# Last FFN by seven block products for gate and up, convolution sums in PSUM, weight lo parts on GpSimd

## The chip, the cores and the metric

The kernel runs on one core of a Trainium2 chip. The metric is the device time of one execution in microseconds. Three executions of the kernel before took 2322.36, 2325.06 and 2325.65 us; their median is 2325.06 us. The engines are called PE (TensorE), DVE (VectorE), ACT (ScalarE), POOL (GpSimd) and SP (SyncE, which issues all DMAs here).

## The reference

A trunk of two layers over 1024 tokens of 1024 channels, all in float32. Layer 0 has a hybrid mixer (gated linear attention beside stick-breaking attention), layer 1 a conformer convolution module; behind each stands a gated FFN of width 2816. Cut to what the change touches:

```python
def conformer_conv(h, w_pw1, b_pw1, w_dw, b_dw, ln_g, ln_b, w_pw2, b_pw2):
    a = h @ w_pw1 + b_pw1
    u = a[..., :D_MODEL] * jax.nn.sigmoid(a[..., D_MODEL:])
    u = depthwise_causal_conv(u, w_dw, width=31) + b_dw
    u = layer_norm(u, ln_g, ln_b)
    return jax.nn.silu(u) @ w_pw2 + b_pw2

def swiglu(h, wg, wu, wd):
    return (jax.nn.silu(h @ wg) * (h @ wu)) @ wd

for layer in range(2):
    h = h + mixer(rms_norm(h, mix_norm[layer]))
    h = h + swiglu(rms_norm(h, ffn_norm[layer]), ffn_w_gate[layer], ffn_w_up[layer], ffn_w_down[layer])
```

(`depthwise_causal_conv`, `layer_norm` and `mixer` stand for several lines of the reference.)

## The kernel before, in words

Every large product is made of three matmuls. A float32 operand is split into a high part, rounded to the format fp32r (a copy on ACT), and a low part, the remainder (a subtraction on DVE); `split` (line 95) does both, `parts` (line 167) does it for a piece of weights, and `mm3` (line 205) adds hi x hi, hi x lo and lo x hi into one PSUM tile. A matmul has 128 rows of the contraction, 128 stationary columns and 512 moving ones.

The tokens are worked in two halves of 512. The residual lies in SBUF as eight token tiles `xres` of 128 x 1024. A norm (`norm_half`, line 142) scales the tokens, transposes them on PE and leaves hi and lo parts with the channels on the partitions, eight blocks of 128 channels ("k").

An FFN of one half of the tokens is a list of steps (`ffn_steps`, line 238). A chunk step takes 128 of the 2816 hidden columns: 24 matmuls for gate (`pg`) and 24 for up (`pu`), then Silu on ACT, the product `s` on DVE (line 261), and its split into `a`. After each group of four chunks two `down` steps (line 211), one for each half of the output columns, multiply the group's activations by `ffn_w_down` and add the PSUM tile `po` to `xres` on DVE (line 230). In the first layer's FFN of the first half the groups have two chunks.

A step is a pair (weights, body). `run` (line 186) traces the weights of a step, that is their DMA, the hi copies and the lo subtractions, one such step ahead of its body. The tile framework then orders the instructions of each engine at build time by a simulated timeline: what is ready and stands earliest in the program goes first, so the matmuls of neighbouring steps can mix. On the chip each engine runs its list in that order.

Layer 1 and the FFNs that surround it are one list of steps, which the last `run` of the kernel gets. For the second half of the tokens the order is: the first pointwise step `p1[0]`, the norm for `f10` (the last FFN's first half), then the other seven pointwise steps and 21 steps of `f10`, between which 32 pieces of the depthwise convolution are spread (`conv_steps`, line 897: eight channel blocks, four pieces each, a piece being up to eight taps, each tap one DVE instruction of line 908 on 128 x 512, accumulating in an SBUF tile `cv`); then six steps of `f10` with the twelve steps of the LayerNorm between them (`layer_norm`, line 915: four for the statistics of the token tiles, eight for transposing back, swish and split), the rest of `f10` but four steps, the four steps of the second pointwise product (`pw2`), the norm for `f11` (the last FFN's second half), the last four steps of `f10`, and `f11`. The stores of the output follow the steps that finish each half.

PSUM has eight buffers of 128 x 512. In layer 1 they are shared out as three of tag "a" (gate, up, pointwise), three of "b" (down) and two of "n" (norms and transposes). Raw weights have two buffers of 128 x 2048, split weights eight of 128 x 1024, for the whole kernel. The bias of the second pointwise product is added to `xres` on POOL (line 963), the only large work POOL has.

The lines that the rows name: L97 hi copies (ACT), L98 lo subtractions (DVE), L146 the norm's scaling, L207 to L209 the three matmuls of `mm3`, L230 the add of `po` to `xres`, L887 the gated pointwise output `u`, L908 a tap, L930 to L936 the LayerNorm's statistics.

Of the kernel before, what the change touches and what calls it, by code (L numbers as in the profile page):

```python
# [25 lines left out]
NF = DFF // P  # L26
EPS = 1e-6
# [12 lines left out]
def trunk(ctx, tc, x, mix_norm, ffn_norm, hy_w_in, hy_w_gate2, hy_b_gate, hy_gla_norm,  # L40
# [8 lines left out]
    raw_p = ctx.enter_context(tc.tile_pool(name="raw", bufs=2))  # L49
    ws_p = ctx.enter_context(tc.tile_pool(name="ws", bufs=8))  # L50
    dram = ctx.enter_context(tc.tile_pool(name="dram", bufs=1, space=DRAM))

# [7 lines left out]
    identr = const.tile([P, P], F32R, name="identr")  # L60
    nc.scalar.copy(identr, ident)
    maskr = const.tile([P, P], F32R, name="maskr")
    hones = const.tile([P, P], F32, name="hones")
    nc.vector.memset(hones, 0.0)
    nc.vector.memset(hones[0:64, 0:64], 1.0 / 64.0)
    nc.vector.memset(hones[64:128, 64:128], 1.0 / 64.0)

    # vectors, 128 channels to a row, transposed on chip into columns
# [34 lines left out]
    small = ctx.enter_context(tc.tile_pool(name="small", bufs=2))  # L103

    def inv_sqrt(y, ss, scale, name):
        """y = 1 / sqrt(ss * scale + eps), by Newton's iteration."""
# [12 lines left out]
    def x_tile(name, dt=F32):  # L119
        return hold.tile([P, 1056], dt, name=name, tag="x", bufs=8)  # L120
# [6 lines left out]
    def norm_stats(xt, junk, name):  # L127
        """1 / RMS of four token tiles."""
# [13 lines left out]
    def norm_half(xt, xn, rs, gcol, ps, pstag, name, muls):  # L142
        """Four token tiles scaled (into xn); returns the transposed hi and lo parts [D chunk, 8, 512]."""
# [11 lines left out]
    def load_cols(w, c0, name, n=256):  # L155
        """n columns of a weight with 1024 rows."""
# [4 lines left out]
    def load_rows(w, r0, n, j, name):  # L161
        """n chunks of 128 rows of a weight with 1024 columns, half j of the columns."""
# [4 lines left out]
    def parts(raw_ap, name, shape=(P, NK, P)):  # L167
        hi = ws_p.tile(list(shape), F32R, name=f"wh_{name}", tag="ws")
        lo = ws_p.tile(list(shape), F32R, name=f"wl_{name}", tag="ws")
        split(hi, lo, raw_ap)  # L170
        return hi, lo

    # A step is a function, or a pair (weights, body) whose weights are traced one such step ahead.
    def interleave(main, filler):
        """The main steps in order, with the filler steps spread evenly behind them."""
# [29 lines left out]
    def mm3(ps, sh, sl, mh, ml, first, last):  # L205
        """ps += s^T m by the three leading products of the hi and lo parts."""
        nc.tensor.matmul(ps, sh, mh, start=first, stop=False)  # L207
        nc.tensor.matmul(ps, sh, ml, start=False, stop=False)  # L208
        nc.tensor.matmul(ps, sl, mh, start=False, stop=last)  # L209
# [803 lines left out]
```

## Time and profile before

| | us |
|---|---|
| median of three executions | 2325.06 |
| lowest and highest | 2322.36, 2325.65 |
| profiled execution, span from the first to the last instruction | 2319.9 |
| PE busy | 2290.3 |
| DVE busy | 1591.3 |
| ACT busy | 922.4 |
| POOL busy | 32.9 |

Of the profiled execution only the span is given, and no time of its own beside it; the span is 5.2 us shorter than the median of the three. "Busy" is time in which an instruction's record is open on the engine. Matmul records overlap, so the spacing of their starts tells more than their length. "Idle before" in a row is the time its engine stood still just before, and the arrow names what ended it.

### The profile page before, as it was taken

How to read it: one execution, taken by the hardware profiler on the slowest of the kernel's cores; microseconds unless marked ns; L12 is line 12 of the kernel's file. 1: busy time of each engine (PE TensorE's matmuls, PEld its weight loads, DVE VectorE, ACT ScalarE, POOL GpSimd, SP SyncE). 2: the span in 40 equal slices, each digit the busy share in tenths (PEclk: the TensorE clock that was granted, in tenths of full speed). 3: DMA queues.
4: the chain of work that ended last, by engine and by line, in shares of the span. 5: the costliest groups of instructions: out<-in, count | busy, mean ns of one | idle time of the engine just before them, and what ended most of it. 6: DMA issues, size and time to landing. Idle time of an engine off the chain costs nothing.

```text
span 2319.9 us, 27940 instructions
## 1 busy us (share of the span) xinstructions
PE 2290.3 (99%) x10866; PEld 1899.1 (82%) x10866; DVE 1591.3 (69%) x2486; ACT 922.4 (40%) x1506; POOL 32.9 (1%) x39
## 2 busy tenths in 40 slices
PE   7999999999999999999999999999999999999999
PEld 6788888788888887788888888888888888888887
DVE  6687764877788656588888856789998545334334
ACT  6465545655565324523222245422222424222221
POOL 0000000000000001000000002000000000000000
PEclk9999999999999999999999999999999999999999
DMA  6254454233343235233222322322322223322322
GB/s 207 97 163 141 167 188 141 76 98 118 100 131 111 68 103 181 73 97 103 91 93 89 109 91 82 109 86 96 109 91 91 91 92 127 109 91 92 108 84 80
DMA packets 206387, 253.74 MB, mean 109 GB/s; under 512 B 8709, under 2 KB 156272, under 8 KB 206254
## 3 DMA queue, kind: packets, MB, share of 16 engines
q1 hardware_dynamic: 206254, 251.95, 33.5%
q8 instruction: 85, 1.39, 0.2%
q14 instruction: 48, 0.39, 0.1%
HBM read 230.95 MB, written 20.97 MB: 109 GB/s over the span
## 4 chain that ended last, share of the span: by engine, by line
PE 95%; DMA 2%; DVE 2%; ACT 1%; issue 0%; SPq 0%; ACTq 0%; DVEq 0%
PE po L207 9%; PE po L209 9%; PE po L208 9%; PE pu L207 7%; PE pu L209 7%; PE pu L208 7%; PE pg L207 7%; PE pg L209 7%; PE pg L208 7%; PE pp L208 2%; PE pp L207 2%; PE pp L209 2%; PE po L652 2%; PE wt L634 1%; PE z L617 1%; PE z L613 1%
## 5 line engine op out<-in xcount | busy, mean ns | idle before, releaser
L908 DVE SCALAR_TENSOR_TENSOR cv<-u,wd,cv 128x512 f32<-128x512 f32 x480 | 358.1, 749 | 9.9
L230 DVE TENSOR_TENSOR xr<-xr,po 128x512 f32<-128x512 f32 x296 | 202.1, 684 | 168.8 <-PE po L209 168.0
L207 PE MATMUL po<-wh_d,a 128*128 128x512 f32 x704 | 277.8, 395 | 1.7 <-DVE xr L230 1.6
L207 PE MATMUL pg<-hh_f,wh_g 128*128 128x512 f32 x704 | 275.8, 392 | 3.6 <-DVE s L260 3.6
L208 PE MATMUL pg<-hl_f,wh_g 128*128 128x512 f32 x704 | 276.6, 393 | 0.0
L209 PE MATMUL pg<-hh_f,wl_g 128*128 128x512 f32 x704 | 275.8, 392 | 0.0
L209 PE MATMUL po<-wh_d,a 128*128 128x512 f32 x704 | 275.5, 391 | 0.0
L208 PE MATMUL pu<-hl_f,wh_u 128*128 128x512 f32 x704 | 275.4, 391 | 0.0
L208 PE MATMUL po<-wl_d,a 128*128 128x512 f32 x704 | 275.2, 391 | 0.0
L209 PE MATMUL pu<-hh_f,wl_u 128*128 128x512 f32 x704 | 275.2, 391 | 0.0
L207 PE MATMUL pu<-hh_f,wh_u 128*128 128x512 f32 x704 | 275.0, 391 | 0.0
L97 ACT CAST wh_g<-raw_g 128x1024 fp32r<-128x1024 f32 x88 | 92.8, 1054 | 348.4 <-PE po L208 226.2
L97 ACT CAST wh_d<-raw_d 128x1024 fp32r<-128x1024 f32 x88 | 92.5, 1053 | 252.0 <-PE pu L208 116.7
L98 DVE TENSOR_TENSOR wl_g<-raw_g,wh_g 128x1024 fp32r<-128x1024 f32 x88 | 107.6, 1223 | 88.0 <-ACT wh_g L97 83.8
L207 PEld LDWEIGHTS po<-wh_d,a 128*128 128x128 f32 x704 | 132.3, 188 | 31.4 <-DVE xr L230 4.0
L207 PEld LDWEIGHTS pg<-hh_f,wh_g 128*128 128x128 f32 x704 | 132.6, 188 | 30.8 <-DVE s L260 3.8
L209 PEld LDWEIGHTS po<-wh_d,a 128*128 128x128 f32 x704 | 132.2, 188 | 27.8
L209 PEld LDWEIGHTS pg<-hh_f,wl_g 128*128 128x128 f32 x704 | 132.7, 189 | 27.0
L208 PEld LDWEIGHTS pu<-hl_f,wh_u 128*128 128x128 f32 x704 | 132.3, 188 | 27.3
L261 DVE TENSOR_TENSOR s<-s,pu 128x512 f32<-128x512 f32 x88 | 60.5, 687 | 137.1 <-PE pu L209 134.5
L208 PEld LDWEIGHTS pg<-hl_f,wh_g 128*128 128x128 f32 x704 | 132.6, 188 | 26.7
L209 PEld LDWEIGHTS pu<-hh_f,wl_u 128*128 128x128 f32 x704 | 132.2, 188 | 27.0
(318 smaller groups left out, 4300.3 us busy)
## 6 DMA issues: line engine op xcount, KB each, us to landing
raw_g<-in_ffn_w_gate_dram SPq DMA_DIRECT2D x44, 1024.0 KB
raw_u<-in_ffn_w_up_dram SPq DMA_DIRECT2D x44, 1024.0 KB
raw_d<-in_ffn_w_down_dram SPq DMA_DIRECT2D x30, 1024.0 KB
raw_p<-in_cv_w_pw_dram SPq DMA_DIRECT2D x16, 1024.0 KB
raw_d<-in_ffn_w_down_dram SPq DMA_DIRECT2D x28, 512.0 KB
raw_wo<-in_hy_w_out_dram SPq DMA_DIRECT2D x8, 1024.0 KB
raw_q<-in_cv_w_pw_dram SPq DMA_DIRECT2D x8, 1024.0 KB
kr<-k_d SPq DMA_DIRECT2D x48, 128.0 KB
```

The lines of the kernel that those rows point to most:

```text
L97: nc.scalar.copy(hi, src)
L98: nc.vector.tensor_sub(lo, src, r32(hi))
L207: nc.tensor.matmul(ps, sh, mh, start=first, stop=False)
L208: nc.tensor.matmul(ps, sh, ml, start=False, stop=False)
L209: nc.tensor.matmul(ps, sl, mh, start=False, stop=last)
L230: nc.vector.tensor_add(xt[i][:, cs], xt[i][:, cs], po)
L261: nc.vector.tensor_mul(s, s, pr[1])
L613: nc.tensor.matmul(z, qs[:, sub(i)], kh[:, s0:s0 + w], start=True, stop=False)
L617: nc.tensor.matmul(z, qs[:, sub(i)], kl[:, s0:s0 + w], start=False, stop=True)
L634: nc.tensor.transpose(pt[:, col:col + P], wrow[bi][:, P * j:P * j + P], ident)
L652: nc.tensor.matmul(po[:, lo_c:256], st["v"][j // 4][:, j % 4, e, :], m[:, 256 * jj + lo_c:256 * jj + 256], start=(last and jj == 0 and m i ...
L908: i = nc.vector.scalar_tensor_tensor(acc, u[:, j:j + TH], wd[:, c, j:j + 1], acc, op0=ALU.mult, op1=ALU.add)
```

## The change

For gate and up of the last FFN the whole product is seen as a 2 x 2 by 2 x 2 block product: blocks of 512 channels, 512 tokens and 1408 hidden columns (11 chunks of 128). b11, b21, b12 and b22 are the normed tokens: the first index is the half of the channels, the second the half of the tokens. It is done with seven block products and additions (the Winograd form of Strassen's method) in place of eight. Two of the seven are on the first half of the tokens and the first half of the hidden columns; they are made in `f10`, which keeps 11 of its 22 chunks. The first of these two products is copied out of PSUM by ACT and stored to DRAM (`m1_d`) while the second is accumulated onto it. The other five come in a new last stage, for eleven pairs of chunks (f and 11 + f), gate and up: `pair_weights` forms four sums of weight blocks on DVE and splits them, `pair_products` makes the five products of 12 matmuls, `pair_down` the down product of the pair. For token tiles 0 to 3 the down product of chunk f was already made in `f10`, so only chunk 11 + f is left.

The new stage has pools of its own; raw and split weights' pools of the earlier stages are closed before it. The order of its steps is gate f, the two down steps of pair f - 1, up f, gate f + 1. At its start `token_sums` and `token_sum4` form the sums of the token blocks on DVE.

In the stage before, the sums of the convolution lie in PSUM (two buffers of tag "cv", and "a" and "b" have two each instead of three), with a copy to SBUF by ACT after the last tap; the lo parts of weights are subtracted on GpSimd; and `f10` being shorter, the convolution's pieces are spread over 16 steps (7 pointwise steps and 9 of `f10`) in place of 28, the LayerNorm's steps over 4 in place of 6. Small tables move into the first stage's pool, and `xres` tiles are 1024 instead of 1056 columns wide.

```diff
-    def split(hi, lo, src, scale=None):
+    def split(hi, lo, src, scale=None, eng=None):
         if scale is None:
             nc.scalar.copy(hi, src)
-            nc.vector.tensor_sub(lo, src, r32(hi))
+            (eng or nc.vector).tensor_sub(lo, src, r32(hi))
...
     def parts(raw_ap, name, shape=(P, NK, P)):
...
-        split(hi, lo, raw_ap)
+        split(hi, lo, raw_ap, eng=weight_engine[0])
...
-    def ffn_steps(l, h, hT, xt, ps, ft, act, use_silu, group):
+    def ffn_steps(l, h, hT, xt, ps, ft, act, use_silu, group, last=NF, early=None):
...
+            if early is not None:
+                for k0 in (0, 4):
+                    for t, (pm, w) in enumerate(zip(pr, ws)):
+                        for k in range(k0, k0 + 4):
+                            mm3(pm, w[0][:, k, :], w[1][:, k, :], hT()[0][:, k, :], hT()[1][:, k, :],
+                                k == 0, k == k0 + 3, skip_group_check=True)
+                        if k0 == 0:
+                            m1 = ft(f"m{t}{nm}")
+                            nc.scalar.copy(m1, pm)
+                            nc.sync.dma_start(early[t, f], m1)
...
+        weight_engine[0] = nc.gpsimd
-        ftp = es.enter_context(tc.tile_pool(name="ft2", bufs=3))
+        ftp = es.enter_context(tc.tile_pool(name="ft2", bufs=4))
...
-            BUFS = {"a": 3, "b": 3, "n": 2}
+            BUFS = {"a": 2, "b": 2, "n": 2, "cv": 2}
...
                 if j0 == 0:
-                    cT[h, c] = cvp.tile([P, TH], F32, name=f"cv{h}{c}", tag="cv")
-                acc = cT[h, c]
+                    sums[h, c] = ps.tile([P, TH], F32, name=f"cs{h}{c}", tag="cv")
+                acc = sums[h, c]
...
+                if j1 == TAPS:
+                    cT[h, c] = cvp.tile([P, TH], F32, name=f"cv{h}{c}", tag="cv")
+                    nc.scalar.copy(cT[h, c], acc)
...
-        f10 = ffn_steps(1, 0, lambda: hT["f10"], xres, ps, ft, act, True, 4)
-        f11 = ffn_steps(1, 1, lambda: hT["f11"], xres, ps, ft, act, True, 4)
+        f10 = ffn_steps(1, 0, lambda: hT["f10"], xres, ps, ft, act, True, 4, NP, m1_d)
...
-               norm_step(0, ffng[1], "f10")] + interleave(p1[1:] + f10[:21], conv_steps(1))
-            + interleave(f10[21:27], ln1) + f10[27:-4] + pw2(1, s1) + [norm_step(1, ffng[1], "f11")]
-            + f10[-4:] + [lambda: store(0, 0), lambda: store(0, 1)]
-            + f11[:-1] + [lambda: store(1, 0), f11[-1], lambda: store(1, 1)])
+               norm_step(0, ffng[1], "f10")] + interleave(p1[1:] + f10[:-8], conv_steps(1))
+            + interleave(f10[-8:-4], ln1) + pw2(1, s1) + [norm_step(1, ffng[1], "f11")] + f10[-4:])
+    weights_es.close()
+    with ExitStack() as es:
+        weight_engine[0] = nc.vector
+        raw_p = es.enter_context(tc.tile_pool(name="raw3", bufs=5))
+        ws_p = es.enter_context(tc.tile_pool(name="ws3", bufs=6))
...
+            BUFS = {"a": 6, "b": 2}
...
+        def token_sums(k):
+            r1, r3, r2 = [whole(b, k, nm) for b, nm in ((b11, "b11"), (b12, "b12"), (b22, "b22"))]
+            nc.vector.tensor_sub(r1, r3, r1)
+            nc.vector.tensor_sub(r3, r2, r3)
+            nc.vector.tensor_sub(r2, r2, r1)
+            for t, r in ((t2, r2), (t3, r3), (t1, r1)):
+                split(t[0][:, k, :], t[1][:, k, :], r)
...
+        def pair_weights(w, t, f):
+            nm = f"{'gu'[t]}{f}"
+            a1, a2 = [load_cols(w, P * c, f"{nm}{c}", P) for c in (f, NP + f)]
+            u = ft(f"m{nm}")
+            nc.sync.dma_start(u, m1_d[t, f])
+            s1 = wp3.tile([P, 4, P], F32, name=f"s1{nm}", tag="w")
+            nc.vector.tensor_add(s1, a2[:, k1, :], a2[:, k2, :])
+            nc.vector.tensor_sub(a2[:, k1, :], a1[:, k1, :], a2[:, k1, :])
+            nc.vector.tensor_sub(a1[:, k1, :], s1, a1[:, k1, :])
+            nc.vector.tensor_sub(a1[:, k2, :], a1[:, k2, :], a1[:, k1, :])
+            s24, s3a = parts(a1, f"s24{nm}"), parts(a2, f"s3a{nm}")
+            ws1 = ws_p.tile([P, NK, P], F32R, name=f"ws1{nm}", tag="ws")
+            split(ws1[:, k1, :], ws1[:, k2, :], s1)
...
+        def pair_products(ws, nm, done):
+            u, s2, s3, s1, s4, a22 = ws
+            pm = lambda i: ps.tile([P, 512], F32, name=f"ps{i}{nm}", tag="a")
+            p1, p2, p3 = pm(1), pm(2), pm(3)
+            product(p1, s2, t2, alone=True)
+            nc.vector.tensor_add(u, u, p1)
+            product(p2, s3, t3)
+            product(p3, s1, t1)
+            v = ft(f"v{nm}")
+            nc.vector.tensor_add(v, u, p3)
+            done(1, 1, p2, v)
+            product(p3, s4, b22, first=False)
+            done(0, 1, p3, u)
+            product(p2, a22, t4, first=False)
+            done(1, 0, p2, u)
...
+                for i in range(NT):
+                    po = ps.tile([P, 512], F32, name=f"po_{i}_{j}", tag="b")
+                    chunks = (0, 1) if i >= 4 else (1,)
...
+        steps, late = [lambda k=k, f=f: f(k) for f in (token_sums, token_sum4) for k in range(4)], []
+        for f in range(NP):
+            mats = pair_steps(1, f)
+            steps += mats[:1] + late + mats[1:]
+            late = [pair_down(1, f, j) for j in range(2)]
```

`done` for gate adds and applies Silu; for up it adds, multiplies by gate's result and splits the product. `product` is 12 matmuls over four channel blocks.

## Rows read from the trace of the kernel before

**Rows 1.** The page: first line, and busy us (share) xinstructions by engine.

```profile
span 2319.9 us, 27940 instructions
PE 2290.3 (99%) x10866; PEld 1899.1 (82%) x10866; DVE 1591.3 (69%) x2486; ACT 922.4 (40%) x1506; POOL 32.9 (1%) x39
```

**Rows 2.** The page: chain that ended last, shares by engine.

```profile
PE 95%; DMA 2%; DVE 2%; ACT 1%; issue 0%; SPq 0%; ACTq 0%; DVEq 0%
```

**Rows 3.** Busy by stretch: us, PE, PEld, DVE, ACT, POOL, PEclk, DMA, GB/s.

```profile
1450.00:1790.00 340.00, 340.00 (x1521) 281.39 (x1520) 299.67 (x411) 102.04 (x127) 1.09 (x5) 1.00 0.30 99
```

**Rows 4.** Timeline, PE, 1968 to 1973.3 (start us, us, engine, operation): first and last.

```profile
1968.00 0.39 PE L207 MATMUL pg<-hh_f,wh_g 128*128 128x512 f32 x1
...
1973.21 0.39 PE L209 MATMUL pg<-hh_f,wl_g 128*128 128x512 f32 x1
```

**Rows 5.** Timeline, 885 to 895, end of the first FFN: adds, matmuls.

```profile
885.16 0.68 DVE L230 TENSOR_TENSOR xr<-xr,po 128x512 f32<-128x512 f32 x1
...
885.90 0.50 PE L207 MATMUL po<-wh_d,a 128*128 128x512 f32 x1 [0.65 <-DVE xr L230]
...
893.69 0.40 PE L209 MATMUL po<-wh_d,a 128*128 128x512 f32 x1
...
894.13 0.69 DVE L230 TENSOR_TENSOR xr<-xr,po 128x512 f32<-128x512 f32 x1 [0.25 <-PE po L209]
```

**Rows 6.** Groups by line, whole span: xcount, busy us, mean ns, idle before.

```profile
L230 DVE TENSOR_TENSOR xr<-xr,po 128x512 f32<-128x512 f32 x296 | 202.1, 684 | 168.8 <-PE po L209 168.0
...
L98 DVE TENSOR_TENSOR wl_g<-raw_g,wh_g 128x1024 fp32r<-128x1024 f32 x88 | 107.6, 1223 | 88.0 <-ACT wh_g L97 83.8 <-PE pg L209 1.9 <-PE pt_f L151 1.5
...
L97 ACT CAST wh_g<-raw_g 128x1024 fp32r<-128x1024 f32 x88 | 92.8, 1054 | 348.4 <-PE po L208 226.2 <-PE pg L208 90.5 <-PE pp L208 15.2
...
L98 DVE TENSOR_TENSOR a<-s,a 128x512 fp32r<-128x512 f32 x88 | 60.2, 685 | 0.5 <-ACT a L97 0.5
```

**Rows 7.** Groups by line, PE, 700 to 880 and, below, 880 to 897.

```profile
L207 PE MATMUL po<-wh_d,a 128*128 128x512 f32 x80 | 32.2, 403 | 0.0
...
L207 PE MATMUL po<-wh_d,a 128*128 128x512 f32 x18 | 7.6, 422 | 1.7 <-DVE xr L230 1.6
```

**Rows 8.** Groups by line, DVE, 1450 to 1790: taps, and lo parts.

```profile
L908 DVE SCALAR_TENSOR_TENSOR cv<-u,wd,cv 128x512 f32<-128x512 f32 x240 | 178.2, 749 | 4.4
...
L101 DVE SCALAR_TENSOR_TENSOR hl_f<-pt_f,vb,hh_f 128x512 fp32r<-128x512 f32 x8 | 5.9, 747 | 0.8 <-ACT hh_f L100 0.7
```

**Rows 9.** Timeline, DVE, 1491 to 1496.

```profile
1491.72 0.74 DVE L908 SCALAR_TENSOR_TENSOR cv<-u,wd,cv 128x512 f32<-128x512 f32 x1
1492.38 0.74 DVE L101 SCALAR_TENSOR_TENSOR hl_f<-pt_f,vb,hh_f 128x512 fp32r<-128x512 f32 x1
1493.04 2.31 DVE L908 SCALAR_TENSOR_TENSOR cv<-u,wd,cv 128x512 f32<-128x512 f32 x3
```

**Rows 10.** Timeline, DVE, 1787 to 1854: LayerNorm, first statistics to last lo parts.

```profile
1787.19 0.70 DVE L930 BATCH_NORM_STATS2 bst<-plt 128x6 f32<-128x512 f32 x1 [0.55 <-PE plt L929]
...
1792.11 0.16 DVE L934 SCALAR_TENSOR_TENSOR lnb<-mv,lrs 128x1 f32<-128x1 f32 x1
...
1852.48 1.29 DVE L98 TENSOR_TENSOR sl<-ls,sh 128x512 fp32r<-128x512 f32 x2 [1.02 <-ACT sh L97]
```

**Rows 11.** Timeline, 1920 to 1934: last add of pw2, scaling of the norm.

```profile
1920.91 0.69 DVE L230 TENSOR_TENSOR xr<-xr,po 128x512 f32<-128x512 f32 x1 [2.03 <-PE po L209]
...
1927.99 5.02 ACT L146 ACTIVATE xn_f<-xr,rs_f 128x512 f32<-128x512 f32 x8 [5.23 <-DVE rs_f L117]
```

**Rows 12.** Timeline, 900 to 920: bias on POOL, a lo part on DVE.

```profile
906.65 11.48 POOL L963 TENSOR_TENSOR xr<-xr,bb 128x1024 f32<-128x1024 f32 x4 [107.17 <-ACT xn_c L146]
...
909.33 3.19 DVE L98 TENSOR_TENSOR wl_wo<-raw_wo,wh_wo 128x1024 fp32r<-128x1024 f32 x1 [1.12 <-ACT wh_wo L97]
```

**Rows 13.** Timeline, 1963 to 1969: a weight load issued, the copy behind it.

```profile
1963.51 0.39 SPq L158 DMA_DIRECT2D raw_u<-in_ffn_w_up_dram  x1
...
1968.90 1.06 ACT L97 CAST wh_u<-raw_u 128x1024 fp32r<-128x1024 f32 x1 [3.01 <-DMA raw_u<-in_ffn_w_up_dram]
```

More of the change, by code (lines that the diff above doesn't have):

```diff
@@ L26 @@
 NF = DFF // P
+NP = NF // 2
 EPS = 1e-6
@@ L119, in x_tile @@
     def x_tile(name, dt=F32):
-        return hold.tile([P, 1056], dt, name=name, tag="x", bufs=8)
+        return hold.tile([P, D], dt, name=name, tag="x", bufs=8)
     def h_tile(name):
@@ L203, in run, with mm3 @@
                 s()
[L205 to L209, printed above, removed]
+    def mm3(ps, sh, sl, mh, ml, first, last, **kw):
+        nc.tensor.matmul(ps, sh, mh, start=first, stop=False, **kw)
+        nc.tensor.matmul(ps, sh, ml, start=False, stop=False, **kw)
+        nc.tensor.matmul(ps, sl, mh, start=False, stop=last, **kw)
     def down(w, r0, acts, xt, tiles, ps, tag, j, name):
@@ L218, in weights @@
             for q in range(0, n, 2):
-                hi, lo = parts(raw[:, q:q + 2, :], f"{name}{j}{q}", (P, 2, 512))
-                wts += [(hi[:, e, :], lo[:, e, :]) for e in range(2)]
+                m = min(2, n - q)
+                hi, lo = parts(raw[:, q:q + m, :], f"{name}{j}{q}", (P, m, 512))
+                wts += [(hi[:, e, :], lo[:, e, :]) for e in range(m)]
             return wts
@@ L242, in weights @@
             if f % 2 == 0:
[L243 to L245 removed]
+                n = P * min(2, last - f)
+                raws["g"] = load_cols(ffn_w_gate[l], P * f, f"g{l}{f}{h}", n)
+                raws["u"] = load_cols(ffn_w_up[l], P * f, f"u{l}{f}{h}", n)
+            c0 = P * (f % 2)
+            return [parts(raws[t][:, :, c0:c0 + P], f"{t}{l}_{f}_{h}") for t in ("g", "u")]
         def chunk(f, ws):
@@ L250, in chunk @@
             for t, w in zip(("g", "u"), ws):
-                pm = ps.tile([P, 512], F32, name=f"p{t}{nm}", tag="a")
-                for k in range(NK):
-                    mm3(pm, w[0][:, k, :], w[1][:, k, :], hT()[0][:, k, :], hT()[1][:, k, :], k == 0, k == NK - 1)
-                pr.append(pm)
+                pr.append(ps.tile([P, 512], F32, name=f"p{t}{nm}", tag="a"))
+                if early is None:
+                    for k in range(NK):
+                        mm3(pr[-1], w[0][:, k, :], w[1][:, k, :], hT()[0][:, k, :], hT()[1][:, k, :],
+                            k == 0, k == NK - 1)
+            if early is not None:
[8 more added lines that the diff above has]
+                            nc.sync.dma_start(early[t, f], m1)
             s = ft(f"s{nm}")
@@ L362, in trunk @@
         t_tile = lambda name, dt=F32: tp.tile([P, 512], dt, name=name, tag="t")
+        identr = gp.tile([P, P], F32R, name="identr")
+        nc.scalar.copy(identr, ident)
+        maskr = gp.tile([P, P], F32R, name="maskr")
+        hones = gp.tile([P, P], F32, name="hones")
+        nc.vector.memset(hones, 0.0)
+        nc.vector.memset(hones[0:64, 0:64], 1.0 / 64.0)
+        nc.vector.memset(hones[64:128, 64:128], 1.0 / 64.0)
         mtmp = ft("mtmp")
@@ L968, in norm_step @@
             return lambda: hT.update({name: norm(h, gcol, name)})
-        def store(h, j):
-            for i in range(4 * h, 4 * h + 4):
-                cs = slice(512 * j, 512 * j + 512)
-                nc.sync.dma_start(xout[i * P:(i + 1) * P, cs], xres[i][:, cs])
         p0 = pw1_steps(0, lambda: hT["c0"])
```

92 lines of the change are left out of this document (77 added, 15 removed).

## The prediction

> **What bounds the kernel now.** I read the busy line first: TensorE is busy 99% of a 2319.9 us span [rows 1]; the profiled execution has no time of its own beside its span, which lies 5.2 us under the median of the runs, 2325.06, so 5.2 is added to every span below. Next the chain that ended last, 95% of it TensorE [rows 2]. Then the stretch in which the second half's convolution runs: TensorE is never idle there, though VectorE is busy 300 of 340 us [rows 3]. So what counts is the issue of matmuls. A record lasts 0.39 us, but they overlap: 24 from 1968.00 to 1973.21 leave 23 gaps of 0.2265 us [rows 4]. This is the price of a matmul, and only work that keeps this pace is free.
>
> **Matmuls removed.** Before, the last FFN has 22 chunks x 2 weights x 2 halves x 24 = 2112 matmuls for gate and up, and 22 x 2 column halves x 8 token tiles x 3 = 1056 for down: 3168. After: the eleven chunks of the first half 11 x 48 = 528, their down 264, eleven pairs of two matrices with five products of 12 matmuls 1320, their down 11 x 2 x (4 x 3 + 4 x 6) = 792: 2904. 264 fewer at 0.2265 us: **-59.8 us**. All of it is on the path; nothing more can come, since TensorE hardly waits now.
>
> **The wait inside the products.** After the third product VectorE must form v = u + p3 before the fourth may add into the same PSUM tile. A row gives each leg [rows 5]: from the last matmul's start to the add's start 894.13 - 893.69 = 0.44, the add 0.69, from an add's end (885.16 + 0.68) to the matmul that waited 0.06. That is 1.19 less the usual 0.23: 0.96. Can other matmuls fill it? The weights of the next step need two of the six weight buffers; the step itself holds five, and one comes free only as the third product ends. So I take it as open: 22 x 0.96 = **+21.1**. Bounds: 0 (down matmuls left over fill it) and 22 x (0.96 + 1.22) = 48, rival B. The fifth product also waits for an add, but the fourth, 12 x 0.2265 = 2.7 us, covers it.
>
> **VectorE in the pairs.** A pair has per matrix four sums of 128x512, two lo parts of 128x1024 and one of 128x512, and five adds; up has three products and three lo parts more; down two lo parts and sixteen adds. With 0.69 and 1.22 us each [rows 6]: 2 x (5 x 0.69 + 2 x 1.22 + 5 x 0.69) + 6 x 0.69 + 2 x 1.22 + 16 x 0.69 = 36.3 us, against 192 matmuls or 43.5 us. So VectorE isn't the bound over a pair, but 83% busy. ScalarE, with six copies of 1.05 us [rows 6] and eight shorter instructions, has under 15 us. In down, token tiles 0 to 3 now take three matmuls, on two PSUM buffers: two tiles turn in 0.45 + 0.44 + 0.69 + 0.06 = 1.64 instead of 1.36 us, 0.5 us a step over four tiles, 22 x 0.5 = 12 if nothing fills it. At the end of the first layer's FFN six-matmul tiles turned on two buffers too: until 880 they waited for nothing, other matmuls standing by, and lost 1.7 us over the 18 groups of three left after that [rows 7]. Here the next first product can stand by: **+4**, bounds 0 and 12.
>
> **The start of the last stage.** The token sums read the second half's norm, and their buffers and the raw weight buffers lie where closed pools lay, so I let them start when the old stage's matmuls are done. First 36 instructions of 0.69 us, 24.7; 16 more (11 us, for the fifth product) hide behind the first four products. Products one to three can follow for the first three of four channel blocks, 27 matmuls or 6.1 us, leaving 18.6; the first pair's weights, 5.9 us of VectorE, go mostly where it waits for ScalarE's copies: together **+20**. Bounds: 10 (half of it beside the last down steps) and 31 (24.7 + 5.9, nothing beside).
>
> **The convolution and the chain behind it.** It had 28 main steps and now 16, of 48 matmuls or 10.9 us each: 174 us, with 248 taps. What VectorE pays for a tap that reads and writes PSUM no row shows. Reading PSUM makes no difference: adds with and without it take 684 and 685 ns, multiply-adds 747 and 749 [rows 6, 8]. So I bound the pitch by 0.66 us (two chains in turn, 1491.72 to 1492.38) and 0.785 ((2.31 - 0.74)/2, three taps of one chain) [rows 9], 164 to 195 us. Fifteen other multiply-adds at 0.66 and 22 adds, products and lo parts at 0.69 make 25 more; the weights' lo parts are gone to GpSimd. It ends 15 to 46 us behind TensorE's sixteenth step. [...] Behind the taps come the LayerNorm, 67 us before (1787.2 to 1853.8), paced by main steps standing ahead of it; four tiles of some 7 us (4.9 for its small instructions alone) and eight swishes of 2 would give 45 [rows 10]. Then pw2, on TensorE; then the last norm: from 1920.91 to the scaled tokens at 1933.0, and eight lo parts, 20 us in all [rows 11]. To cover these there are eight steps left of the first half's FFN, 360 matmuls or 81.6 us. At the low pitch 15 + 45 + 20 = 80: covered, **0**; I take this since the two PSUM accumulators give two chains whenever VectorE is behind. Bounds: 0, and 46 + 67 + 20 - 81.6 = 51.
>
> **Smaller things.** GpSimd adds 128x1024 in 11.48/4 = 2.87 us; a VectorE instruction with both inputs in SBUF took 3.19 instead of 1.22 meanwhile [rows 12]. With the taps in PSUM only some 50 such are left in that stage, and a step gives GpSimd 5.7 of 10.9 us. With one PSUM buffer less for each tag: **+1**, bounds 0 and 8. SyncE issues 22 stores and 22 loads of a partial product more and, in smaller pieces, 44 + 44 weight loads in the pairs; a store waits for a ScalarE copy and holds back the weight loads queued behind it, but these run a step ahead and a load landed 5.4 us after its issue [rows 13]: 0, or 5.4 us for each of the 22 matrices if the lead were gone. The tail: the last pair's down waits for its multiply and split: **+2**.
>
> Sum: -59.8 + 21.1 + 4 + 20 + 0 + 1 + 2 = **-11.7**: span 2308.2, time **2313.4 us**.
>
> **Rivals.** (A) Slower: the convolution is the bound. Half as many steps carry all its taps, so VectorE has 189 to 220 us of work in 174. It decides once taps, LayerNorm and last norm together pass the 81.6 us of cover by 17 us; midway, a pitch of 0.72 and 60 us of LayerNorm, it is 30 + 60 + 20 - 81.6 = 28, at most 51: 2341, up to 2364. For it: VectorE was busy 88% there with the taps spread over 28 steps. Against: the weights' lo parts, two of 1.22 us a step [rows 6], left it. [...] (B) The lo part of the next step's weights gets its buffer at the same moment as v gets its input, and stands earlier in the program: if it goes first, every wait is 1.22 us longer, 22 x 1.22 = 27: 2340. (C) Much faster: leftover down matmuls fill most of the waits (5 instead of 21.1) and half of the token sums run beside the last steps (10): 2287. For it: down matmuls with others standing by waited for nothing [rows 7]. That the change doesn't remove what it says I give no chance: the loops fix the counts.
>
> **Chances.** Forecast 0.42, A 0.25, B 0.15, C 0.18. About 0.2%, 4.65 us, is what a measurement can tell, so the bounds are 2320.4 and 2329.7. The forecast's own range is 2298 to 2325; some 0.33 of its 0.42 is faster, 0.06 the same, 0.03 slower. With C: faster 0.51; A and B add 0.06 to the same: 0.12; slower 0.37. The range reaches from 2283 to 2360, leaving out the lower part of C and the end of A.
>
> **What would show it.** 2904 matmuls in the last FFN at 0.2265; TensorE idle 22 times, about 0.96 us, before the fourth product, released by the add v; one gap of some 20 us before the first products, ended by VectorE; no gap over 2 us between the last tap and pw2. A gap before the LayerNorm's transposes or pw2 makes A right, waits of 2 us before the fourth product with a lo part just ahead of v make B right, a busy TensorE throughout C. Wrong altogether: GpSimd or a DMA as the releaser of TensorE's long waits.

## The result: slower, and the profile after

| | before | changed kernel |
|---|---|---|
| median, us | 2324.6 (4 runs) | 2404.52 (4 runs) |
| lowest and highest, us | 2322.36, 2325.65 | 2402.16, 2405.17 |
| span of the profiled execution, us | 2319.9 | 2400.2 |

The ratio is 1.0346, its 95% interval 1.0331 to 1.0361. The forecast was 2313.4 us with a range up to 2360, so sign and range were both wrong.

The page of the changed kernel, first line and busy line, against [rows 1]:

```profile
span 2400.2 us, 27984 instructions
PE 2272.1 (95%) x10602; PEld 1854.3 (77%) x10602; DVE 1676.9 (70%) x2674; ACT 934.6 (39%) x1550; POOL 393.9 (16%) x195
```

The matmul records fell from 10866 to 10602, by just the 264 of the prediction. TensorE's share fell from 99% to 95%: it now waits. Where, the windows of the changed kernel show; the columns are those of [rows 3]: us, PE, PEld, DVE, ACT, POOL, granted clock, DMA share, GB/s.

```profile
900.00:1600.00 700.00, 670.53 (x3004) 548.26 (x3003) 467.37 (x670) 239.62 (x334) 300.02 (x147) 0.99 0.27 89
1600.00:1700.00 100.00, 100.00 (x444) 82.60 (x443) 98.10 (x142) 37.31 (x51) 44.74 (x19) 1.00 0.41 142
1700.00:1800.00 100.00, 85.09 (x383) 69.47 (x382) 47.63 (x119) 37.26 (x60) 31.10 (x14) 0.90 0.22 72
1800.00:1880.00 80.00, 55.52 (x218) 40.33 (x217) 56.15 (x88) 28.40 (x45) 7.30 (x4) 0.83 0.23 72
1880.00:2350.00 470.00, 446.11 (x1898) 353.07 (x1897) 336.49 (x472) 110.79 (x142) 0.00 (x0) 1.00 0.25 76
```

Only one of these windows keeps TensorE full, that of the convolution's later half; there VectorE is busy 98.10 of 100 us. A busy sum hides part of a loss, since each record lasts 0.39 us and the pitch is 0.2265 [rows 4]. So I added up, over all matmuls, the time from one start to the next beyond 0.2267 us (0.13 for a transpose; eight in a row, 0.27 us each, take 1.03 us from 1747.99 on in the changed kernel, 0.11 from start to start). Before, that is within 3 us of nothing in every stretch from 896 us to 2310. In the changed kernel it is 36.7 us in the pointwise steps (932 to 1050 and 1412 to 1578), 18.8 at the last LayerNorm (1700 to 1752), 34.3 at the start of the last stage (1796 to 1880) and 48.9 in the pairs (1880 to 2385): 138.7. Less 59.8 for the matmuls saved that gives 78.9 of the 80.3 us by which the span grew.

What ended those waits, in the groups of TensorE's instructions of the changed kernel (operation, out<-in, shapes, count, busy us, mean ns, then the idle time just before them and its releasers), one after another for 932 to 1580, 1690 to 1760, 1796 to 1880 and 1880 to 2390:

```profile
L204 PE MATMUL pp<-hh_c,wh_p 128*128 128x512 f32 x256 | 103.5, 404 | 24.0 <-ACT sg L907 24.0
L204 PE MATMUL pg<-hh_f,wh_g 128*128 128x512 f32 x178 | 69.9, 393 | 3.0 <-ACT sg L907 3.0
...
L953 PE MATMUL plt<-ident,cv 128*128 128x128 f32 x26 | 5.8, 371 | 10.2 <-ACT lx L960 10.1
L967 PE MATMUL pls<-ident,lx 128*128 128x128 f32 x32 | 5.8, 331 | 4.6 <-ACT lx L960 4.5
...
L204 PE MATMUL ps1g<-tt,wh_s24g 128*128 128x512 f32 x4 | 3.0, 752 | 15.6 <-ACT wh_s24g L89 14.0 <-ACT tt L89 1.6
L204 PE MATMUL ps3g<-hh_f,wh_s24g 128*128 128x512 f32 x3 | 2.1, 684 | 5.2 <-DVE vg L1091 5.2
...
L205 PE MATMUL po<-wl_dp,ap 128*128 128x512 f32 x255 | 100.9, 396 | 8.7 <-DVE wl_dp L90 8.7
L204 PE MATMUL ps3u<-hh_f,wh_s24u 128*128 128x512 f32 x44 | 18.4, 418 | 10.5 <-DVE vu L1091 10.4
L204 PE MATMUL ps3u<-tt,ws1u 128*128 128x512 f32 x44 | 18.3, 416 | 4.8 <-ACT ws1u L89 4.8
L206 PE MATMUL ps3u<-tt,ws1u 128*128 128x512 f32 x44 | 18.2, 414 | 1.7 <-DVE ws1u L90 1.7
```

The reader is to see four different releasers: the sigmoid of the pointwise step (a PSUM buffer that isn't free), the LayerNorm's scaling (another PSUM buffer), the first weights of the last stage, and in the pairs three late operands beside the sum v that was forecast.

### The profile page after: what moved, and what is told of

It is laid out like the page before. It is cut to its first block, busy times and chain, and to the rows that moved or that the text cites. A ratio compares the mean times of both kernels' runs of the same rounds, so it can differ in the third digit from the quotient of the medians.

```text
span 2400.2 us, 27984 instructions
## 1 busy us (share of the span) xinstructions
PE 2272.1 (95%) x10602; PEld 1854.3 (77%) x10602; DVE 1676.9 (70%) x2674; ACT 934.6 (39%) x1550; POOL 393.9 (16%) x195
## 5 line engine op out<-in xcount | busy, mean ns | idle before, releaser
L929 DVE SCALAR_TENSOR_TENSOR cs<-u,wd,cs 128x512 f32<-128x512 f32 x480 | 350.6, 752 | 9.8
L204 PE MATMUL po<-wh_d,a 128*128 128x512 f32 x440 | 172.5, 395 | 4.5 <-DVE xr L228 4.1
L205 PE MATMUL pg<-hl_f,wh_g 128*128 128x512 f32 x440 | 173.6, 395 | 0.0
L206 PE MATMUL pg<-hh_f,wl_g 128*128 128x512 f32 x440 | 172.8, 393 | 0.0
L205 PE MATMUL pu<-hl_f,wh_u 128*128 128x512 f32 x440 | 172.7, 392 | 0.0
L206 PE MATMUL pu<-hh_f,wl_u 128*128 128x512 f32 x440 | 172.4, 392 | 0.0
L205 PE MATMUL po<-wl_d,a 128*128 128x512 f32 x440 | 172.3, 392 | 0.0
L206 PE MATMUL po<-wh_d,a 128*128 128x512 f32 x440 | 171.7, 391 | 0.0
L204 PE MATMUL pp<-hh_c,wh_p 128*128 128x512 f32 x256 | 103.5, 404 | 24.0 <-ACT sg L907 24.0
L205 PE MATMUL po<-wl_dp,ap 128*128 128x512 f32 x264 | 104.5, 396 | 8.7 <-DVE wl_dp L90 8.7
L204 PE MATMUL po<-wh_dp,ap 128*128 128x512 f32 x264 | 103.4, 398 | 4.3 <-ACT ap L89 2.7
L206 PE MATMUL po<-wh_dp,ap 128*128 128x512 f32 x264 | 103.4, 392 | 0.0
```

The source lines that it names most:

```text
L204: nc.tensor.matmul(ps, sh, mh, start=first, stop=False, **kw)
L205: nc.tensor.matmul(ps, sh, ml, start=False, stop=False, **kw)
L206: nc.tensor.matmul(ps, sl, mh, start=False, stop=last, **kw)
L929: i = nc.vector.scalar_tensor_tensor(acc, u[:, j:j + TH], wd[:, c, j:j + 1], acc, op0=ALU.mult, op1=ALU.add)
```

## The experiments

My theory: the operations are as cheap as forecast, and the loss is four shortages of buffers or cover, each in its own stretch. Its rivals: taps in PSUM or the work on GpSimd are dear in themselves, or the seven products are bound to lose.

**1. Each half of the change alone.** The kernel before with the change's supporting parts only (sums in PSUM, two buffers for each tag, low parts on GpSimd), and the changed kernel without them:

```diff
+        weight_engine[0] = nc.gpsimd
...
-            BUFS = {"a": 3, "b": 3, "n": 2}
+            BUFS = {"a": 2, "b": 2, "n": 2, "cv": 2}
...
```

> The kernel before with only the supports of the change: convolution in PSUM, two buffers each for tags a, b, n and cv, lo parts on GpSimd; no seven products. Theory: the 16 pointwise steps lose 1.9 to 2.3 us each as in the changed kernel, 30 to 37 us, and nothing else is lost since the convolution has its 28 steps: 2355 to 2362. Rival (the supports cost nothing, all losses come with the block products): 2325.

> The changed kernel without its supports: convolution in SBUF, three PSUM buffers for a and b, lo parts on VectorE. Theory: the pointwise steps lose nothing (-37), but VectorE has two lo parts of 1.22 us more in each of the 16 steps that carry the taps, 39 us, and TensorE waits for the LayerNorm 40 to 60 us instead of 19; start of the last stage and pairs as they are: 2400 to 2420. Rival (the supports weren't needed): only the -37 shows, 2368.

The supporting parts alone: 2368.18 us against 2322.37, 1.0198 (1.0168 to 1.0228), some 46 us lost on the kernel before, 6 more than the theory allowed; 44 of them, by the sum over starts, lie between 896 and 1600. The pointwise row of this run, 932 to 1600, waits for the sigmoid as in the changed kernel:

```profile
L209 PE MATMUL pp<-hh_c,wh_p 128*128 128x512 f32 x256 | 103.3, 404 | 23.5 <-ACT sg L889 23.5
```

The seven products alone: 2401.43 us, 1.0341 (1.0311 to 1.0371). There the pointwise steps lose nothing; 54 us are lost around the LayerNorm, and 83 in the last stage, as in the changed kernel. Groups of TensorE, 896 to 1800, in the run with the products alone:

```profile
L949 PE MATMUL plt<-ident,cv 128*128 128x128 f32 x64 | 13.8, 343 | 42.7 <-DVE cv L928 29.4 <-ACT lx L956 13.3
```

29.4 us of it wait for a tap: with 16 steps in place of 28 beside it, the convolution on VectorE is late. So rival A was a true danger of the products; the supporting parts remove it and cost as much in the pointwise steps: 2404.5 with, 2401.4 without.

**2. The pointwise steps.** Only the order of the two products of a step is changed, so that the half that the sigmoid reads comes first:

```diff
...
-                for t, w in enumerate(ws):
+                for t in (1, 0):
+                    w = ws[t]
...
```

> The changed kernel, with the two products of a pointwise step in the other order: the gate's half first, so that its sigmoid runs beside the second product. Theory (two PSUM buffers of tag a instead of three make each of the 16 steps wait for sigmoid and gated product, 36.7 us in all): these waits go. In the first half of the tokens that is worth 17 us. In the second half TensorE comes 15 to 20 us earlier to the LayerNorm, where it waits for the convolution on VectorE, so part of it comes back there (18.8 us lost now, up to 35 then): 2368 to 2388. Rival (GpSimd's lo parts, 2.4 instead of 1.2 us, come late for these steps): the waits stay, 2404.

2365.96 us, 1.0188 (1.0159 to 1.0218): 38.6 us less than the changed kernel, 2 us better than the theory's range and more than the 36.7 lost there. Its row, 932 to 1580, against 24.0 us of idle time above:

```profile
L204 PE MATMUL pp<-hh_c,wh_p 128*128 128x512 f32 x256 | 100.4, 392 | 0.0
```

With two buffers, the next step's first product needs one that the step before still holds; in the old order both are held until the sigmoid of the second has run. The timeline of the changed kernel at one such wait, in order of starts: last product matmul, ScalarE's other work, the sigmoid, the next step's first matmul, and the eighth after it.

```profile
952.60 0.39 PE L206 MATMUL pp<-hh_c,wl_p 128*128 128x512 f32 x1
...
957.10 1.03 ACT L89 CAST wh_p<-raw_p 128x1024 fp32r<-128x1024 f32 x1
958.03 0.68 ACT L907 ACTIVATE sg<-pp,vb 128x512 f32<-128x512 f32 x1
958.76 0.80 PE L204 MATMUL pp<-hh_c,wh_p 128*128 128x512 f32 x1 [3.53 <-ACT sg L907]
...
962.03 0.39 PE L206 MATMUL pp<-hh_c,wl_p 128*128 128x512 f32 x1
```

The sigmoid starts 5.4 us after the last matmul of its step, behind other ScalarE work. This is one of two long waits; the other 14 of the 16 sigmoids start 1.2 us after the last matmul, behind one copy of a weight's high part, and TensorE waits 0.67 to 1.55 us for them. In the new order the sigmoid runs beside the second product. None of the gain came back at the taps: VectorE had slack before them (467 of 700 us busy in the first window above).

**3. The pairs.** One more buffer for split weights in the last stage, one less for raw ones:

```diff
-        raw_p = es.enter_context(tc.tile_pool(name="raw3", bufs=5))
-        ws_p = es.enter_context(tc.tile_pool(name="ws3", bufs=6))
+        raw_p = es.enter_context(tc.tile_pool(name="raw3", bufs=4))
+        ws_p = es.enter_context(tc.tile_pool(name="ws3", bufs=7))
```

> The changed kernel with seven split-weight buffers instead of six in the last stage (and four raw ones instead of five, to fit). Theory (the waits of 4.4 us in each pair, for the third and fourth product of up and for the lo part of down's weights, come from split weights that get their buffer late): about half of the 48 us go, 2375 to 2390. Rival (VectorE, 75% busy in that stage, is late by itself, or four raw buffers are too few): no change or slower, 2400 to 2410.

2362.68 us, 1.0174 (1.0145 to 1.0204): 41.8 us less, where about half of the 48.9 lost in the pairs was expected. The view of the tile s1g in the changed kernel, made once for each pair (count, shortest/median/longest ns, first and last start):

```profile
L1071 DVE TENSOR_TENSOR s1g<-raw_g x11: 691/692/693, 1840.0 to 2316.4; 128x512 f32<-128x512 f32 x11
```

(2316.4 - 1840.0)/10 is 47.6 us a pair, 4.1 above the 192 x 0.2265 = 43.5 of its matmuls. The window 1900 to 2300, in the changed kernel and with seven buffers:

```profile
1900.00:2300.00 400.00, 378.72 (x1617) 299.68 (x1617) 287.94 (x405) 93.50 (x120) 0.00 (x0) 1.00 0.26 80
```

```profile
1900.00:2300.00 400.00, 399.22 (x1748) 326.78 (x1747) 310.45 (x442) 102.85 (x129) 0.00 (x0) 1.00 0.28 85
```

And TensorE's group behind v with seven buffers, 1880 to 2390:

```profile
L204 PE MATMUL ps3u<-hh_f,wh_s24u 128*128 128x512 f32 x44 | 17.1, 389 | 0.0
```

TensorE is all but full (by the sum over starts 10 us are still lost in the pairs), and even the wait for v is gone (10.5 us above). What fills it the timelines show: the end of the third product of up and the first matmul of the fourth, in the changed kernel and with seven buffers.

```profile
2128.21 0.39 PE L206 MATMUL ps3u<-tt,ws1u 128*128 128x512 f32 x1
2129.53 0.50 PE L204 MATMUL ps3u<-hh_f,wh_s24u 128*128 128x512 f32 x1 [0.94 <-DVE vu L1091]
```

```profile
2102.47 0.39 PE L206 MATMUL ps3u<-tt,ws1u 128*128 128x512 f32 x1
2102.69 0.39 PE L204 MATMUL po<-wh_dp,ap 128*128 128x512 f32 x1
...
2104.51 0.39 PE L206 MATMUL po<-wh_dp,ap 128*128 128x512 f32 x1
2104.73 0.39 PE L204 MATMUL ps3u<-hh_f,wh_s24u 128*128 128x512 f32 x1
```

With seven buffers nine down matmuls stand between the two, in ten of the eleven pairs; in the changed kernel none are left by then.

**4. Taps in SBUF beside GpSimd.** The sums go back to SBUF, the low parts stay on GpSimd:

```diff
-            BUFS = {"a": 2, "b": 2, "n": 2, "cv": 2}
+            BUFS = {"a": 3, "b": 3, "n": 2}
...
-                    sums[h, c] = ps.tile([P, TH], F32, name=f"cs{h}{c}", tag="cv")
-                acc = sums[h, c]
+                    cT[h, c] = cvp.tile([P, TH], F32, name=f"cv{h}{c}", tag="cv")
+                acc = cT[h, c]
...
```

> The changed kernel with the convolution's sums back in SBUF and the PSUM buffers of before (3/3/2), the low parts of the weights still on GpSimd. Nothing of the computation is left out. Against the run with both parts undone (2401.4 us, where 46.7 us were lost ahead of the LayerNorm's transposes, 29.4 of them on VectorE's taps) it moves the low parts alone. Theory: those taps were late because VectorE was full, so that the 1.22 us of each low part of the weights taken off it bring the taps in: the loss ahead of the transposes falls to 12 to 20 us, and the time is 2365 to 2380 us. Rival: taps that read two operands from SBUF are held up by GpSimd working beside them, longer than 749 ns each, and the gain is under 10 us: 2392 to 2403 us.

2442.49 us, 1.0510 (1.0496 to 1.0524): 41 us slower than with the low parts on VectorE, worse than the rival's figure. VectorE's groups, 896 to 1800, in this run, in the changed kernel (taps in PSUM) and in the run without supporting parts (taps in SBUF, GpSimd busy 32 of 904 us):

```profile
L929 DVE SCALAR_TENSOR_TENSOR cv<-u,wd,cv 128x512 f32<-128x512 f32 x480 | 500.2, 1069 | 8.2
```

```profile
L929 DVE SCALAR_TENSOR_TENSOR cs<-u,wd,cs 128x512 f32<-128x512 f32 x480 | 350.6, 752 | 9.8
L90 DVE TENSOR_TENSOR a<-s,a 128x512 fp32r<-128x512 f32 x32 | 63.8, 1993 | 14.8 <-ACT a L89 14.8
```

```profile
L928 DVE SCALAR_TENSOR_TENSOR cv<-u,wd,cv 128x512 f32<-128x512 f32 x480 | 346.1, 747 | 5.9
L90 DVE TENSOR_TENSOR a<-s,a 128x512 fp32r<-128x512 f32 x32 | 21.9, 684 | 0.0
```

A tap with both large operands in SBUF takes 747 ns alone and 1069 beside GpSimd, with its sum in PSUM 752 beside GpSimd. The low part of an activation, whose two inputs stay in SBUF, goes from 684 to 1993. So with the sums in SBUF the low parts on GpSimd cost 41 us; with the sums in PSUM the taps keep their pace beside them. By what mechanism GpSimd holds up an instruction with two inputs in SBUF was not shown. The fourth combination, sums in PSUM and low parts on VectorE, was not run.

This run also parts the buffers from GpSimd: with the low parts there but three buffers, the pointwise products wait 0.6 us for sigmoids in place of 24.0 (they wait 8.5 for the slower VectorE instead).

**5. The start of the last stage.** Three orders of its pools, with the same buffers. The first two put the token sums' tiles over memory that is free early; the second also moves the work tile w3 ahead of all (the diff is the first's; gap3 is an empty tile that keeps the places):

```diff
+        wp3 = es.enter_context(tc.tile_pool(name="w3", bufs=1))
         ap3 = es.enter_context(tc.tile_pool(name="act3", bufs=6))
+        sp3 = es.enter_context(tc.tile_pool(name="s3", bufs=4))
+        gap3 = es.enter_context(tc.tile_pool(name="gap3", bufs=1))
...
         fp3 = es.enter_context(tc.tile_pool(name="ft3", bufs=6))
-        sp3 = es.enter_context(tc.tile_pool(name="s3", bufs=4))
-        wp3 = es.enter_context(tc.tile_pool(name="w3", bufs=1))
         tp3 = es.enter_context(tc.tile_pool(name="t3", bufs=1))
```

> The changed kernel with the pools of the last stage opened in another order, the same buffers: those of the token sums (the work tiles and the two big combination tiles) lie where the convolution's tiles of the stage before lay, which are done early, in place of where its gated activations lay, which are read to its end. Theory: the token sums waited for that memory; they now run beside the last down steps of the old stage, and the 34.4 us that TensorE lost at the start of the last stage fall to 8 to 20 us: 2378 to 2391 us. Rival 1: the weights of the first pair (through ScalarE and VectorE) or the last residual additions set the start, and the sums come early for nothing: 2398 to 2406 us. Rival 2: the sums take VectorE's time from the residual additions and the normalisation that the last down steps wait for, and the gain is lost there: 2395 to 2415 us.

> The placement run again, with the work tile of the weight combinations (the single buffer w3) first among the last stage's pools, over raw weights that are used up early, in place of over the eighth split-weight buffer of the old stage. In the placement run the first token sum came 11 us earlier than in the changed kernel, but the first weight combination 11 us later (1850.59 against 1839.97) and with it the first product 14 us later. Theory: that tile's memory was what the first combination waited for; with it free, first product within some 3 us of the last residual addition, and 8 to 20 us less than the changed kernel: 2383 to 2397 us. Rival: VectorE's order, not memory, holds the combination back (it does the token sums first), and the time stays at 2394 to 2400 us as in the placement run.

2397.78 us (1.0321, 1.0307 to 1.0335) and 2398.51 us (1.0325, 1.0309 to 1.0341): 6 to 7 us each, where 8 to 26 were expected. In both the token sums now start 20 us ahead of the last old matmul, but the first weight sum still comes some 6 us behind it and the first product 18, so the memory of the sums and of w3 was not what held it. The timeline of the changed kernel shows what it waits for: last old matmul, first weight load, first token sum, first weight sum, its split, first product.

```profile
1834.07 0.39 PE L206 MATMUL po<-wh_d,a 128*128 128x512 f32 x1
1834.53 1.01 SPq L153 DMA_DIRECT2D raw_g<-in_ffn_w_gate_dram  x2
1835.10 3.09 DVE L1040 TENSOR_TENSOR b<-hh_f,hl_f 128x512 f32<-128x512 f32 x5
1839.97 0.69 DVE L1071 TENSOR_TENSOR s1g<-raw_g 128x512 f32<-128x512 f32 x1 [1.18 <-issue]
1847.37 1.04 ACT L89 CAST wh_s24g<-raw_g 128x1024 fp32r<-128x1024 f32 x1 [3.04 <-DVE raw_g L1074]
1848.46 0.79 PE L204 MATMUL ps1g<-tt,wh_s24g 128*128 128x512 f32 x1 [14.01 <-ACT wh_s24g L89]
```

SyncE issues the load only when the last old matmul is done; load, sums and split then take 13.9 us. The third order puts the raw weights over the convolution's old memory, the combination tiles over the old weights:

```diff
-        raw_p = es.enter_context(tc.tile_pool(name="raw3", bufs=5))
+        tp3 = es.enter_context(tc.tile_pool(name="t3", bufs=1))
         ws_p = es.enter_context(tc.tile_pool(name="ws3", bufs=6))
         ap3 = es.enter_context(tc.tile_pool(name="act3", bufs=6))
+        raw_p = es.enter_context(tc.tile_pool(name="raw3", bufs=5))
+        wp3 = es.enter_context(tc.tile_pool(name="w3", bufs=1))
         fp3 = es.enter_context(tc.tile_pool(name="ft3", bufs=6))
         sp3 = es.enter_context(tc.tile_pool(name="s3", bufs=4))
-        wp3 = es.enter_context(tc.tile_pool(name="w3", bufs=1))
-        tp3 = es.enter_context(tc.tile_pool(name="t3", bufs=1))
```

> The changed kernel with the last stage's pools opened in a third order, the same buffers: the raw weights, the work tile and the 128x512 work tiles over memory of the convolution, the combination tiles first, over the old weights. In the changed kernel the first load of weights of the last stage is issued at 1834.53, just after the old stage's last matmul (1834.46), and in the run with w3 first at 1842.97, again just after it, though the token sums came 13 us earlier. Theory: the loads wait until the old weights' memory, under the new raw weights, is read to the end, and load, combination and split (14 us from the issue to the first product) stand behind that: with the raw weights elsewhere, the load is issued over 15 us before the last old matmul, the first product comes within 8 us of it in place of 14, and the time is 2384 to 2396 us. Rival: VectorE is the bound (its sums, 52 of 0.69 us, and the residual additions), or the sums now wait for the old weights' memory: the first product still comes 12 us or more behind, 2397 to 2408 us.

2395.13 us, 1.0313 (1.0299 to 1.0328): 9.4 us less, at the theory's dear end; its four executions (2393.8 to 2399.0) reach into the rival's figure, and its interval overlaps those of the other two orders. Its timeline: the load, a down matmul, the last old matmul and the first product.

```profile
1824.69 1.01 SPq L153 DMA_DIRECT2D raw_g<-in_ffn_w_gate_dram  x2
...
1828.84 0.80 PE L204 MATMUL po<-wh_d,a 128*128 128x512 f32 x1 [2.81 <-DVE xr L228]
...
1843.77 0.39 PE L206 MATMUL po<-wh_d,a 128*128 128x512 f32 x1
1845.93 0.51 PE L204 MATMUL ps1g<-tt,wh_s24g 128*128 128x512 f32 x1 [1.78 <-ACT tt L89]
```

The load is 19 us ahead of the last old matmul and the first product 2.2 us behind it in place of 14.4; it now waits for a split token sum. So the load was what the first product waited for; but the 12.2 us won there arrive only in part, since the last old matmul itself comes later (1843.77 against 1834.07, and as late in the first two orders). The old stage's down matmuls, for one, now wait 2.81 us for a residual addition, with VectorE at token sums beside it. By the sum over starts, 1796 to 1880, TensorE still loses 27.4 us, against 34.4 in the changed kernel and 28 in each of the first two orders. That VectorE is the next limit there is likely, but no run tests it.

**6. Together.** The three repairs (order of the products, seven buffers, placement of the token sums), and the same with the LayerNorm spread over six steps:

```diff
-               norm_step(0, ffng[1], "f10")] + interleave(p1[1:] + f10[:-8], conv_steps(1))
-            + interleave(f10[-8:-4], ln1) + pw2(1, s1) + [norm_step(1, ffng[1], "f11")] + f10[-4:])
+               norm_step(0, ffng[1], "f10")] + interleave(p1[1:] + f10[:-10], conv_steps(1))
+            + interleave(f10[-10:-4], ln1) + pw2(1, s1) + [norm_step(1, ffng[1], "f11")] + f10[-4:])
```

> The changed kernel with three repairs at once: the pointwise products in the other order, seven buffers of split weights in the last stage (four raw ones), and the last stage's pools in the order of the placement run. Theory: the three losses lie in different stretches and add: 2404.5 less 38.6 (other order) less 41.8 (seven buffers) less 12 to 26 (placement) is 2298 to 2312 us, below the kernel before (2322 to 2325 us). Rival: what one repair gains another has already (seven buffers also helped the first pair), and placement brings nothing more: 2320 to 2328 us, no better than before.

> The three repairs, and the last LayerNorm spread over six steps of the feed-forward layer in place of four, the convolution over two fewer. Theory: the 18.8 us lost at the LayerNorm are waits of its transposes for the normalisation of the tile two before (a chain of some 6.2 us for each token tile on VectorE and ScalarE, with too few matmuls between them), so that more steps between them take 8 to 15 us off the run with the three repairs. Rival: VectorE is full up to the last tap, so that the LayerNorm can't begin earlier and the steps moved into it are only taken from the convolution's cover: within 5 us of that run, or up to 10 us slower.

2315.42 us, 0.9964 (0.9951 to 0.9978), between the two figures. The gains add: 89.1 us together, where alone they were 38.6, 41.8 and 6.7; the kernel is now 0.4% faster than before. Six steps make it worse, 2331.26 us, 1.0037 (1.0024 to 1.0049), by 15.8 us where the rival allowed 10: groups of TensorE, 1590 to 1760:

```profile
L954 PE MATMUL plt<-ident,cv 128*128 128x128 f32 x28 | 7.2, 412 | 27.1 <-ACT cv L936 13.9 <-ACT lx L961 13.2
```

The LayerNorm can't begin before the last tap, behind which L936 copies the sum. Then w3 first, and with it a second pair of buffers for the LayerNorm's transposes:

```diff
-                    pt = ps.tile([P, 512], F32, name=f"plt{h}{i}{j}", tag="n")
+                    pt = ps.tile([P, 512], F32, name=f"plt{h}{i}{j}", tag=("n", "cv")[i % 2])
```

> The three repairs, with w3 first in the placement as in the run beside this one. Theory: the 13.5 us that TensorE still loses ahead of the first gate product fall by 5 to 12 us: 2303 to 2311 us. Rival: VectorE is full there (45 of 50 us), and only the order of its work changes: 2312 to 2318 us.

> The run beside this one, and the LayerNorm's transposes of every second token tile go to the two PSUM buffers of the convolution, which are free by then. Theory: with two buffers the transposes of a tile wait until both buffers of the tile before are read, so that four chains of some 6.2 us stand one behind another; with four buffers two chains run at once, and of the 19.6 us lost ahead of plt and pls 8 to 14 go: 8 to 14 us below the run beside this one. Rival: the chains share one VectorE and the reads of ScalarE, and the in-order queue of TensorE is held by pls in place of plt: less than 4 us below.

w3 first: 2317.83 us, 0.9979 (0.9971 to 0.9988), nothing gained, as the rival said. The buffers: 2307.96 us, 0.9935 (0.9923 to 0.9948), 9.9 less, as the theory said. Groups of TensorE, 1640 to 1760, against 10.6 us with w3 first:

```profile
L954 PE MATMUL plt<-ident,cv 128*128 128x128 f32 x26 | 4.7, 324 | 1.7 <-ACT lx L961 1.6
```

Last, this with the third order of the pools:

> The last run with all repairs (2308.0 us), with the pools in the order of the run beside this one in place of the placement of the token sums. Theory: 19.9 us are lost there ahead of the first gate product, and 8 to 14 of them go: 2294 to 2301 us. Rival: the sums that wait for the old weights' memory take the place of the load: 2304 to 2314 us.

2305.49 us, 0.9928 (0.9915 to 0.9942): within the rival's figure; the 2.5 us to the run before it lie inside their intervals. The wait for the first weights, 16.9 us in that run, is gone, and shorter waits for the token sums' parts and other operands have come in its place. It is the fastest median found, 17.7 us or 0.7% under the kernel before. Of its span 11 us are still lost at the LayerNorm, 26 at the start of the last stage and 9 in the pairs, by the sum over starts.

## Why the prediction was wrong, step by step

- **Matmuls removed, -59.8**: right. 264 records fewer, and the pitch is 0.2265 wherever nothing waits.
- **"With one PSUM buffer less for each tag: +1, bounds 0 and 8"**: the first step that failed, 36.7 us in its place. I had counted the instructions that GpSimd slows (3.19 us for 1.22 [rows 12]) but walked through no step that turns on two buffers. The pointwise step was to be walked: two products into two buffers, a sigmoid that needs the second, and ScalarE busy with other work ahead of it. Experiment 2 shows the place, experiment 1 shows it without the seven products.
- **The wait inside the products, +21.1, and down, +4**: 48.9 us. The price of a wait for v was nearly right: 1.32 us from start to start (experiment 3), 1.09 beyond the pitch, against 0.96. But it came 11 times, in up alone; in ten of eleven pairs gate's was filled, since six down matmuls stand by there. Not forecast were the weights: split too late for want of a buffer, they hold up `ws1u` and `wl_dp` too. The prediction named the cause (six buffers, five held) and used it only to leave the wait for v open. With seven TensorE is busy 399.22 of 400 us, and leftover down matmuls fill the waits: rival C's picture, had the buffers been there.
- **The start of the last stage, +20**: 34.3, beyond its bound of 31. It was priced as VectorE's work with the weights beside it. The load behind the last old matmul (experiment 5) put the weight chain on the path ahead of the products, and a slower clock (0.83 granted in the window 1800 to 1880) came on top. With the load early 27.4 us remain, behind split token sums and residual additions; how much of that is VectorE's work and how much the clock stays open.
- **The convolution, 0**: the taps were right. They take 752 ns in PSUM against 749 in SBUF [rows 8]. The TensorE-full window 1600 to 1700 shows that they kept up. **The LayerNorm behind it** cost 18.8 us, inside the bounds 0 and 51: I held its chain covered by the matmuls of eight steps without asking whether they can run meanwhile. In TensorE's list the transposes stood ahead of them, and it sat idle for 14.8 us (10.2 and 4.6 above) while they waited for two buffers; experiment 6 took almost half of that back by buffers alone (from 19.7 to 10.8 us, by the sum over starts).
- **The tail, +2**: 0.8 after 2385; nothing hangs on it.
- **Rivals.** A, the convolution as the bound, is what the products do without the supporting parts (experiment 1), and not what happened here. B, the lo part ahead of v, didn't show: a wait for v cost 1.09 us, not 2.2. C failed for a buffer. GpSimd released none of the long waits; a DMA stands behind one, the first weights, where the row names ScalarE.

## What to carry to other kernels

A buffer given away is priced by walking one full step of every stage that shares it: who holds it, who frees it, and what that engine does just before. An idea that saves matmuls on a full TensorE can lose more in such places than it saves; before it is dropped, the waits are read by their releasers, since an order of two products, one buffer, a borrowed pair of buffers and another order of pools turned 1.0346 into 0.9935 here. Memory of a new stage should put what the first loads need where the old one ends early.

## What the hardware showed unasked

TensorE's clock fell after some of the waits, so that such a wait cost more than its idle time. Windows of the changed kernel around one pointwise wait, in the columns of the windows above:

```profile
955.00:958.70 3.70, 0.23 (x2) 0.00 (x0) 0.00 (x0) 3.70 (x7) 0.50 (x1) 0.94 0.03 9
958.80:961.50 2.70, 2.70 (x7) 2.13 (x8) 2.01 (x3) 1.99 (x3) 2.57 (x3) 0.50 0.00 0
962.00:970.00 8.00, 8.00 (x37) 6.61 (x36) 0.00 (x0) 1.05 (x1) 3.65 (x2) 1.00 0.00 1
```

TensorE was idle for 3.5 us, and the matmuls after that ran at a granted clock of 0.50, then at 1.00. From the first matmul behind the wait to the eighth after it (the last two rows of the timeline in experiment 2) it took 3.27 us in place of 8 x 0.2265 = 1.81: the wait of 3.53 us cost 1.5 more. Not every wait did this: after one of 1.55 us the clock was still 1.00.

```profile
999.17 0.50 PE L204 MATMUL pp<-hh_c,wh_p 128*128 128x512 f32 x1 [1.55 <-ACT sg L907]
```

```profile
999.00:1002.00 3.00, 2.83 (x12) 2.34 (x13) 2.78 (x4) 0.12 (x1) 2.15 (x2) 1.00 0.39 139
```

Before the change the clock was 1.00 in the window of [rows 3]; the forecast priced every wait at its idle time alone.

GpSimd took 2406 ns for a low part of 128x1024 (33 of them, 896 to 1800), 1223 on VectorE [rows 6]; the prediction's nearest row had 2.87 us [rows 12]:

```profile
L90 POOL TENSOR_TENSOR wl_u<-raw_u,wh_u 128x1024 fp32r<-128x1024 f32 x33 | 79.4, 2406 | 43.7 <-ACT wh_u L89 43.7
```
